# A two-layer hybrid mixer and mixture-of-experts block: the largest expert's three blocks apart, and the first loads of both mixers in places of their own

## The chip, the cores and the metric

The kernel runs on one core of one Trainium2 chip. The metric is the device time of one execution in microseconds (us). Before the change three runs gave 2003.07, 2004.57 and 2011.16 us, a median of 2004.57 us. A difference of about 0.5% (10 us) is what a measurement of this kernel can tell from no change.

## The reference, cut to what matters

512 latent tokens and 256 context tokens of width 1024 go through two layers. Each layer first runs a token mixer: adaptive-norm modulation, one projection into a short convolution and a recurrent head group, one output projection. Then it runs a mixture of 32 experts, of which each token uses two.

```python
for l in range(DEPTH):                                   # 2 layers
    mod = silu(c) @ w_ada[l] + b_ada[l]                  # w_ada[l]: 1024 x 6144
    h = modulate(rms_norm(x, norm_w[l, 0]), mod[0], mod[1])
    y, _, _ = token_mixer(h, w_in[l], ...)               # h @ w_in[l], 1024 x 4096, first
    x = x + mod[2] * (y @ w_out[l])
    h2 = modulate(rms_norm(x, norm_w[l, 1]), mod[3], mod[4])
    f = hier_moe(h2, ..., w_e_gu[l], w_e_down[l])        # per expert: 1024 x 1024 and 512 x 1024
    x = x + mod[5] * f
return rms_norm(x, final_norm_w)
```

The context tokens take the same path in the first layer, so that it routes 768 tokens and the second layer 512. All of it is float32.

## The kernel before, in words

**Order of work.** `run` (L1678) does, per layer, `mixer` (L565), the routing (`route`, L862) and the experts (`moe`, L1469). Each engine has its own queue of instructions. Tile's planner orders them by its own model of their durations, except inside a `manual_schedule` of an engine, where the program's order holds. SP's queue issues most loads and waits in order: a load whose place is not yet free holds up all that stand behind it.

**First layer's start.** `setup` (L40) brings seven small tensors into one 128x128 tile `rows` with seven loads on SP's queue (L47). `norm_first` (L286) loads six tiles of 128 tokens into two places `xin` on ACT's queue, normalises each (ACT's square, POOL's power, DVE's scaling), transposes it on PE (L298) and copies it to `XT`. `ada_step` (L199), eight times, loads 1 MB of `w_ada` on SP's queue into one of three places `adaw` (L215) and multiplies it on PE (L217). From the sum come the modulation's factors `mA` (L241, L242). Then `nat(6)` loads four pieces of `w_in` (0.5 MB each, L317, two places `raw`), and `split_w` (L312) splits each in two: ACT rounds it to the upper part (L319), and POOL or DVE subtracts for the lower part (L322). `modulated` (L264) writes a tile of tokens, again as upper and lower part, into `HA` (input rows 0 to 511) and `HB` (512 to 1023): ACT the upper (L274), DVE the exact value (L278), POOL the difference (L283). `val` (L590) multiplies it by the split weights with 24 matmuls (`proj_N`, L337 to L346) in three kinds per input block: upper by upper, upper by lower weight, lower input by upper weight, block after block. I call these 6 x 24 matmuls the value stage.

**Second layer's start.** The same stage, but the tokens are `X` plus two rows of expert results each, which `combine` (L1615) loads on SP's queue (L1622) and adds on DVE (L1626). DVE keeps the program's order here. Two weight pieces are split with DVE, the other two, loaded between the first `combine` loads, with POOL (L605 to L615).

**Experts.** An expert's weights are six chunks of 1 MB, four of `w_e_gu` and two of `w_e_down`. `ring` (L1168) hands out places in turn from the list `slots`: six of `ra`, eleven of `r0` to `r3`, less one for `m5s` in the first layer, so 16. Three experts are static; the others come by rank of their load in the fixed `order` (L1657). `rooms` (L1653) says for how many tokens a rank has room; `units` (L1456) cuts that into blocks of 128, 64 and 32 tokens. In the first layer rank 0 has 320 (two blocks of 128, one of 64), rank 1 has 192, rank 2 has 128, ranks 3 to 5 have 96, ten ranks 64, thirteen 32. `moe` takes rank after rank: `take_rows` gathers the tokens (POOL's indirect load, PE's transposes), `chunks` does the gate and up matmuls chunk by chunk for all the rank's blocks (L1227 for 128, L1231 else), `end` (L1437) the activation and the down matmuls (L1284, L1296) block by block, and the scatter. PE keeps the program's order. A chunk's place is free when PE has used it for the rank's last block.

```python
order = [[6, 16, 7, 17, 0, 18, 19, 1, 20, 21, 2, 22, 8, 3, 23, 9, ...
def ring(self, n=6):
    pool, name = self.slots.pop(0)
    self.slots.append((pool, name))
```

Of the kernel before, what the change touches and what calls it, by code (L numbers as in the profile page):

```python
# [9 lines left out]
F32 = mybir.dt.float32  # L10
# [9 lines left out]
D = 1024  # L20
# [13 lines left out]
class Backbone:  # L34
# [4 lines left out]
    def setup(self, consts, tmp, ps, dram, stp):  # L39
# [3 lines left out]
        nc.gpsimd.memset(rows, 0.0)  # L43
        q = nc.sync

        def put(r, src):
            q.dma_start(rows[r:r + src.shape[0], :], src)  # L47

        put(0, io["c"].rearrange("a (r j) -> (a r) j", j=128))
        put(8, io["c_ctx"].rearrange("(r j) -> r j", j=128))  # L50
        put(16, io["norm_w"].rearrange("a b (r j) -> (a b r) j", j=128))
        put(48, io["conv_w"].rearrange("a b (r j) -> (a b r) j", j=128))
        put(72, io["conv_norm_w"].rearrange("a (r j) -> (a r) j", j=128))
        put(80, io["hg_lb"].rearrange("a b (r j) -> (a b r) j", j=128))
        put(96, io["hg_norm_w"])
# [143 lines left out]
    def ada_step(self, l, g, k, st, pool, ps, q, bufs):  # L199
# [14 lines left out]
        w = pool.tile([128, 2048], F32, name="adaw", bufs=bufs)  # L214
        q.dma_start(w, io["w_ada"][l, 128 * k:128 * k + 128, 2048 * g:2048 * g + 2048])  # L215
# [47 lines left out]

    def modulated(self, l, i, H, src, pool):  # L264

# [19 lines left out]
    def norm_first(self, H, pool, ps):  # L285

        nc, io = self.nc, self.io
        XT = pool.tile([128, 8, TOK], F32, name="XT")
        for i in range(6):
            xt = pool.tile([128, D], F32, name="xin", bufs=2)  # L290
            src = io["x"][0, i * 128:(i + 1) * 128, :] if i < 4 else io["ctx"][0, (i - 4) * 128:(i - 3) * 128, :]
            nc.scalar.dma_start(xt, src)
            xn = self.normalise(xt, pool)
            for h in range(2):
                pt = ps.tile([128, 512], F32, name="pS", bufs=2)
                for j in range(4):
                    k = 4 * h + j
                    nc.tensor.transpose(pt[:, 128 * j:128 * j + 128], xn[:, 128 * k:128 * k + 128], self.ident)  # L298
# [1527 lines left out]
```

## Time and profile before

| what | value |
|---|---|
| median of three runs | 2004.57 us |
| the profiled execution's own time | 1997.62 us |
| its span, first to last instruction | 1995.8 us |
| busy, share of the span: PE | 1714.4 us, 86% |
| DVE, ACT, POOL | 919.1 us, 456.8 us, 394.1 us |
| mean granted TensorE clock | 0.936 |
| moved by DMA | 542.35 MB, mean 272 GB/s |

The profiled execution is a single one; its time is 6.95 us under the median of the runs. Its span lies 1.8 us under its own time. PE is busy for most of the span, but a busy PE is not PE at its peak, and stages differ: in the expert stages the DMA engines are full, in the mixers they are not. So one reads a stage at a time: which engine or queue runs through it, and which wait ends last. In the rows below a timeline's bracket is the idle time of that engine before the row and what ended it.

### The profile page before, as it was taken

How to read it: one execution, taken by the hardware profiler on the slowest of the kernel's cores; microseconds unless marked ns; L12 is line 12 of the kernel's file. 1: busy time of each engine (PE TensorE's matmuls, PEld its weight loads, DVE VectorE, ACT ScalarE, POOL GpSimd, SP SyncE). 2: the span in 40 equal slices, each digit the busy share in tenths (PEclk: the TensorE clock that was granted, in tenths of full speed). 3: DMA queues.
4: the chain of work that ended last, by engine and by line, in shares of the span. 5: the costliest groups of instructions: out<-in, count | busy, mean ns of one | idle time of the engine just before them, and what ended most of it. 6: DMA issues, size and time to landing. Idle time of an engine off the chain costs nothing. (4 is left out here: it accounts for less than half of the span.)

```text
span 1995.8 us, 33492 instructions
## 1 busy us (share of the span) xinstructions
PE 1714.4 (86%) x13488; PEld 1098.7 (55%) x13488; DVE 919.1 (46%) x2141; ACT 456.8 (23%) x897; POOL 394.1 (20%) x308
## 2 busy tenths in 40 slices
PE   5999899999967999988876799898987898888875
PEld 2766778898844344433322588777764344334342
DVE  4425355634664233222322637666565434355444
ACT  3512223323121122122211533323320100101011
POOL 1501221121112111111110623222212111111110
PEclk8999899999977999998988799999997999999998
DMA  7376563262479979999997422113569989999995
GB/s 276 98 256 229 165 207 97 76 232 83 164 277 416 418 280 390 418 417 417 418 419 319 163 74 65 54 43 91 192 247 375 418 346 400 418 417 417 417 418 246
DMA packets 141512, 542.35 MB, mean 272 GB/s; under 512 B 17393, under 2 KB 66719, under 8 KB 85416
## 3 DMA queue, kind: packets, MB, share of 16 engines
q1 hardware_dynamic: 118408, 466.17, 59.2%
q10 hardware_dynamic: 15040, 55.08, 8.0%
q0 software_dynamic: 7904, 18.90, 2.5%
q8 instruction: 108, 1.77, 0.4%
q14 instruction: 52, 0.43, 0.1%
HBM read 530.95 MB, written 15.96 MB: 274 GB/s over the span
## 5 line engine op out<-in xcount | busy, mean ns | idle before, releaser
L1231 PE MATMUL acc<-w,xT 128*32 128x256 f32 (+1 forms) x3360 | 385.4, 459 | 55.0 <-DMA w<-in_w_e_gu 45.9
L1231 PEld LDWEIGHTS acc<-w,xT 128*32 128x32 f32 (+1 forms) x3360 | 128.5, 121 | 258.3 <-issue 176.3
L322 POOL TENSOR_TENSOR hilo<-raw,hilo 128x1024 fp32r<-128x1024 f32 x64 | 157.5, 2467 | 446.8 <-ACT hilo L319 398.7
L333 PE MATMUL acc<-HA,hilo 128*128 128x384 f32 (+1 forms) x960 | 209.1, 361 | 0.0
L333 PE MATMUL acc<-HB,hilo 128*128 128x384 f32 (+1 forms) x960 | 206.3, 358 | 0.0
L333 PEld LDWEIGHTS acc<-HA,hilo 128*128 128x128 f32 x960 | 172.1, 193 | 16.5 <-issue 4.2
L333 PEld LDWEIGHTS acc<-HB,hilo 128*128 128x128 f32 x960 | 174.3, 194 | 9.5 <-issue 0.8
L345 PE MATMUL acc<-hilo,HA 128*128 128x512 f32 x504 | 131.7, 414 | 13.0 <-ACT HA L274 4.4
L1251 ACT COPY au<-acc 128x256 f32<-128x256 f32 (+1 forms) x69 | 31.2, 452 | 461.6 <-PE acc L1231 439.3
L1190 POOL DMA_INDIRECT xb<-h,idx x63 | 64.2, 1019 | 331.5 <-PE pS L1212 301.8
L345 PE MATMUL acc<-hilo,HB 128*128 128x512 f32 x504 | 125.8, 398 | 3.7 <-DVE hilo L322 3.3
L345 PEld LDWEIGHTS acc<-hilo,HA 128*128 128x128 f32 x504 | 98.1, 199 | 41.6 <-POOL HA L283 5.8
L319 ACT CAST hilo<-raw 128x1024 fp32r<-128x1024 f32 x80 | 83.5, 1049 | 128.2 <-PE acc L345 41.5
L345 PEld LDWEIGHTS acc<-hilo,HB 128*128 128x128 f32 x504 | 94.3, 190 | 29.0 <-issue 4.2
L1182 POOL DMA_INDIRECT yb<-ys,idx x39 | 38.9, 998 | 338.3 <-DVE ys L1298 288.0
L389 DVE TENSOR_TENSOR Q<-Q,Dk 128x256 f32<-128x256 f32 (+1 forms) x144 | 89.8, 653 | 28.8 <-PE pA L435 12.2
L1214 DVE COPY xT<-pS 128x256 f32<-128x256 f32 (+1 forms) x79 | 42.1, 544 | 124.4 <-PE pS L1212 123.6
L1275 DVE SCALAR_TENSOR_TENSOR au<-w,gt,au 32x256 f32<-32x256 f32 (+2 forms) x102 | 58.6, 577 | 60.1 <-ACT au L1274 57.1
L1258 DVE TENSOR_TENSOR hT<-pS,hT 128x128 f32<-128x128 f32 (+1 forms) x69 | 22.9, 340 | 134.3 <-ACT hT L1257 133.9
L384 DVE TENSOR_TENSOR K<-K,Dk 128x768 f32<-128x768 f32 x64 | 72.9, 1139 | 21.8 <-ACT tmp L401 18.3
L1296 PE MATMUL ada<-w,hT 128*32 128x256 f32 (+1 forms) x624 | 67.1, 442 | 5.6 <-issue 4.3
L1334 PE MATMUL ada<-w,hT 128*32 128x256 f32 (+1 forms) x608 | 61.2, 444 | 11.6 <-DVE hT L1259 11.4
(376 smaller groups left out, 2283.8 us busy)
## 6 DMA issues: line engine op xcount, KB each, us to landing
w<-in_w_e_gu SPq DMA_DIRECT2D x242, 1024.0 KB
w<-in_w_e_down SPq DMA_DIRECT2D x121, 1024.0 KB
adaw<-in_w_ada ACTq DMA_DIRECT2D x40, 1024.0 KB
raw<-in_w_in SPq DMA_DIRECT2D x64, 512.0 KB
adaw<-in_w_ada SPq DMA_DIRECT2D x8, 1024.0 KB
raw<-in_w_out SPq DMA_DIRECT2D x16, 512.0 KB
HA<-in_w_e_gu SPq DMA_DIRECT2D x6, 1024.0 KB
h<-SG SPq DMA_DIRECT2D x10, 512.0 KB
```

The source lines that it names most:

```text
L319: nc.scalar.copy(W[:, 0], w)
L322: eng.tensor_sub(W[:, 1], w, W[:, 0].bitcast(F32))
L333: nc.tensor.matmul(o, W[:, wi, k, :], H[k // 4][:, k % 4, hi, t], start=k == 0 and wi == hi, stop=k == 7 and wi == 1)
L345: nc.tensor.matmul(pa, H[k // 4][:, k % 4, hi, t], W[k // 2][:, wi, k % 2, :], start=k == ks[0] and wi == hi, stop=k == ks[-1] and hi == 1)
L384: nc.vector.tensor_tensor(half(Kv, TOK, 0, kn, b), half(Kv, TOK, 0, kn, b), vw(Dv, b, [[2 * b, n], [TOK - b, 2], [0, b]]), op=OP.mult)
L389: nc.vector.tensor_tensor(o, o, vw(Dv, (TOK + b) * d, [[2 * b, qn // (2 * b)], [0, b]]), op=OP.mult)
L1190: self.nc.gpsimd.indirect_dma_start(out=xb, out_offset=None, in_=rows, in_offset=bass.IndirectOffsetOnAxis(ap=idx, axis=0), bounds_check=r ...
L1214: nc.vector.tensor_copy(t[:, :n].rearrange("p a b -> p (a b)"), pt[:, :128 * n])
L1231: nc.tensor.matmul(pg[kind * u:kind * u + kind, :w], xT[k], gu[:, k % 2, w * u:w * u + w], start=st, stop=sp)
L1275: nc.vector.scalar_tensor_tensor(ms[pr, :o], self.m5s[pr, 0, c], g0[pr], ms[pr, :o], op0=OP.mult, op1=OP.add)
L1296: nc.tensor.matmul(py[kind * u:kind * u + kind, :w], hT[k], dn[k // 2][:, k % 2, w * u:w * u + w], start=k == 0, stop=k == 3)
L1334: nc.tensor.matmul(py[pr, :w], hT[k], dn[k // 2][:, k % 2, c], start=k == 0, stop=k == 3)
```

## The change

- `setup`: the seven small tensors are put in one 128x128 array outside the kernel, and one load on ACT's queue brings it.
- First layer's start: the six token tiles get a place each, and the eight pieces of `w_ada` too: six in the memory that later holds `HA` and `HB`, two others. The four pieces of `w_in` get places as well: two in `raw`, two in `SG`. All are issued on SP's queue in one written order: tiles 0 and 1, the eight pieces of `w_ada`, the four of `w_in`, tiles 2 to 5. Tiles 2 to 5 are normalised between the modulations instead of ahead of `ada_step`. DVE and POOL subtract in turn.
- Second layer's start: the four pieces of `w_in` are loaded ahead of all `combine` loads, and DVE splits all four ahead of the first addition. For the first tile DVE, not POOL, subtracts the `HA` half.
- `val`: per half of the input first the eight matmuls with the upper input, then the four with the lower.
- Experts: in the first layer's `order` rank 0 stands three times, one block each, with two ranks between (18 and 19, then 20 and 21), and rank 1 and what follows come later. Its six places are kept out of `slots` until its third block is done.
- `down_here` (second layer only): the result buffer taken is the first that no open group uses, instead of the first of the list.

```diff
-        put(0, io["c"].rearrange("a (r j) -> (a r) j", j=128))
...
-        put(96, io["hg_norm_w"])
+        nc.scalar.dma_start(rows, io["small"])
...
-            nc.gpsimd.tensor_sub(H[h][:, :, 1, sl], mh, H[h][:, :, 0, sl].bitcast(F32))
+            (nc.gpsimd if h else eng or nc.gpsimd).tensor_sub(H[h][:, :, 1, sl], mh, H[h][:, :, 0, sl].bitcast(F32))
...
-    def proj_N(self, W, H, i, ps, group=range(4)):
+    def proj_N(self, W, H, i, ps, group=range(4), high=False):
...
+        ms = [(k, hi, wi) for k in ks for hi, wi in ((0, 0), (0, 1), (1, 0))]
+        if high:
+            ms.sort(key=lambda m: (m[0] // 4, m[1]))
...
+            def early():
+                w = [SG[:, 2 * u - 4:2 * u - 2, :] if u > 1 else
+                     wp.tile([128, 2, 512], F32, name="raw", bufs=self.raw_bufs) for u in range(4)]
+                for u in range(4):
+                    nc.sync.dma_start(w[u], win[256 * u:256 * u + 256, 512 * 6:512 * 7].rearrange("(k p) f -> p k f", p=128))
+                return w
...
+                    with tc.manual_schedule(engines={mybir.EngineType.SP}):
+                        for i in range(2):
+                            nc.sync.dma_start(xin[i], self.token_tile(i))
+                        for k in range(8):
+                            self.ada_load(0, 0, k, aw[k], nc.sync)
+                        ew = early()
+                        for i in range(2, 6):
+                            nc.sync.dma_start(xin[i], self.token_tile(i))
+                    for i in range(2):
+                        self.norm_first(i, xin[i], XT, p0, ps)
                     ast = {}
                     for k in range(8):
-                        self.ada_step(0, 0, k, ast, p0, ps, nc.sync, 3)
+                        self.ada_step(0, 0, k, ast, p0, ps, None, 2, aw[k])
                     self.ada_cols(0)
-                    W = nat(6)
+                    W = [self.split_w(None, wp, True, nc.vector if u % 2 else nc.gpsimd, ew[u]) for u in range(4)]
+                    inputs()
                     for i in range(6):
                         self.modulated(0, i, H, lambda k: XT[:, k, 128 * i:128 * i + 128], p0)
+                        if i + 2 < 6:
+                            self.norm_first(i + 2, xin[i + 2], XT, p0, ps)
                         val(W, i)
                 else:
-                    W = nat(6, range(2), nc.vector)
+                    inputs()
+                    ew = early()
...
                     with tc.manual_schedule(engines={mybir.EngineType.DVE}):
+                        W = [self.split_w(None, wp, True, nc.vector, w) for w in ew]
...
-                            if i == -2:
-                                W += nat(6, range(2, 4), nc.gpsimd)
...
-    def ring(self, n=6):
+    def ring(self, n=6, keep=None):
...
-            self.slots.append((pool, name))
+            (self.slots if keep is None else keep).append((pool, name))
...
-            self.YB.append(self.YB.pop(0))
+            busy = [id(self.into[k]) for k in self.groups if k != kind]
+            self.YB.append(self.YB.pop([id(t) in busy for t in self.YB].index(False)))
...
+        order, units, ends = self.order[l], [], []
+        for n, r in enumerate(order):
+            k, us = order[:n].count(r), self.units(l, r)
+            ends.append(r not in order[n + 1:])
+            units.append(us[k:] if ends[n] else us[k:k + 1])
...
+                if not ends[n]:
+                    kept[r] = []
+                ws[r] = self.load_expert(e, self.ring(keep=kept.get(r)))
...
+            if ends[n]:
+                self.slots += kept.pop(order[n], [])
...
-    order = [[6, 16, 7, 17, 0, 18, 19, 1, 20, 21, 2, 22, 8, 3, 23, 9, 4, 24, 10, 5, 25, 11, 12, 26, 13, 14, 27, 15, 28],
+    order = [[6, 16, 7, 17, 0, 18, 19, 0, 20, 21, 0, 22, 1, 23, 8, 2, 24, 9, 3, 10, 25, 4, 11, 5, 26, 12, 13, 14, 27, 15, 28],
```

## Rows read from the trace of the kernel before

**Rows 1.** Windows of the start: busy us (instructions) per engine, clock, DMA share, GB/s.

```profile
2.00:4.00 2.00, 0.00 (x0) 0.00 (x0) 0.00 (x0) 0.94 (x1) 0.00 (x0) 1.00 0.71 276
...
10.00:20.00 10.00, 9.20 (x33) 3.67 (x33) 6.26 (x35) 3.65 (x7) 1.59 (x3) 1.00 0.97 378
```

**Rows 2.** SP's queue at the start, timeline: start us, us, instruction.

```profile
0.72 0.39 SPq L215 DMA_DIRECT2D adaw<-in_w_ada  x1
...
8.35 25.35 SPq L215 DMA_DIRECT2D adaw<-in_w_ada  x7
```

**Rows 3.** PE at the first layer's start, timeline.

```profile
23.93 1.10 PE L298 MATMUL pS<-ident,xn 128*128 128x128 f32 x8
...
39.09 1.38 PE L217 MATMUL ada<-adaw,sT 128*32 128x512 f32 x8 [2.88 <-DMA adaw<-in_w_ada]
...
46.82 1.22 PE L345 MATMUL acc<-hilo,HA 128*128 128x512 f32 x2 [4.45 <-ACT HA L274]
...
82.66 2.88 PE L345 MATMUL acc<-hilo,HA 128*128 128x512 f32 x12
85.38 2.88 PE L345 MATMUL acc<-hilo,HB 128*128 128x512 f32 x12
```

**Rows 4.** DVE between the last adaptive weights and the modulation, timeline.

```profile
42.58 1.22 DVE L322 TENSOR_TENSOR hilo<-raw,hilo 128x1024 fp32r<-128x1024 f32 x1
43.72 2.31 DVE L241 TENSOR_SCALAR mA<-mc 128x16 f32<-128x16 f32 x1
```

**Rows 5.** Windows of the first value stage, columns as in rows 1.

```profile
47.00:56.00 9.00, 5.69 (x13) 3.66 (x13) 9.00 (x15) 7.05 (x16) 6.18 (x4) 0.65 0.22 60
...
62.00:89.00 27.00, 27.00 (x122) 22.42 (x121) 13.92 (x32) 17.69 (x41) 16.70 (x17) 1.00 0.25 80
```

**Rows 6.** Windows of the first layer's expert stage, columns as in rows 1.

```profile
592.00:700.00 108.00, 93.16 (x834) 44.51 (x827) 39.34 (x122) 18.14 (x39) 21.34 (x20) 0.90 1.01 413
...
710.00:740.00 30.00, 29.81 (x174) 13.17 (x172) 12.34 (x21) 8.57 (x16) 6.01 (x6) 1.00 0.51 187
...
780.00:790.00 10.00, 10.00 (x92) 4.00 (x94) 3.36 (x6) 1.65 (x4) 3.12 (x4) 1.00 0.80 288
790.00:1070.00 280.00, 232.89 (x1664) 92.19 (x1658) 77.45 (x155) 54.17 (x108) 41.60 (x41) 0.93 1.01 418
```

**Rows 7.** PE around the largest expert, timeline.

```profile
678.26 3.60 PE L1227 MATMUL pA<-w,xT 128*128 128x512 f32 x8
...
685.22 1.94 PE L1231 MATMUL acc<-w,xT 128*64 128x512 f32 x8
...
715.54 7.13 PE L1284 MATMUL acc<-w,hT 128*128 128x512 f32 x16 [0.19 <-ACT hT L1246]
...
734.53 1.93 PE L1231 MATMUL acc<-w,xT 128*32 128x256 f32 x32
...
741.70 1.93 PE L1296 MATMUL ada<-w,hT 128*32 128x256 f32 x32 [1.50 <-issue]
```

**Rows 8.** SP's expert loads in the full-rate part, timeline: four chunks of an expert each.

```profile
910.17 9.07 SPq L1163 DMA_DIRECT2D w<-in_w_e_gu  x4
...
926.39 9.47 SPq L1163 DMA_DIRECT2D w<-in_w_e_gu  x4
```

**Rows 9.** The second layer's start, all engines, timeline.

```profile
1094.23 2.54 DVE L322 TENSOR_TENSOR hilo<-raw,hilo 128x1024 fp32r<-128x1024 f32 x2 [1.65 <-ACT hilo L319]
...
1104.08 6.12 POOL L322 TENSOR_TENSOR hilo<-raw,hilo 128x1024 fp32r<-128x1024 f32 x2 [0.17 <-ACT hilo L319]
...
1105.86 5.42 DVE L1626 TENSOR_TENSOR X<-X,y 128x1024 f32<-128x1024 f32 x2 [1.16 <-DMA y<-yb]
...
1108.22 1.22 PE L345 MATMUL acc<-hilo,HA 128*128 128x512 f32 x2 [1.44 <-ACT HA L282]
...
1112.46 4.63 PE L345 MATMUL acc<-hilo,HA 128*128 128x512 f32 x10 [3.02 <-POOL HA L283]
...
1123.29 3.00 PE L345 MATMUL acc<-hilo,HA 128*128 128x512 f32 x12
```

More of the change, by code (lines that the diff above doesn't have):

```diff
@@ L342, in proj_N @@
         ks = [2 * u + a for u in group for a in range(2)]
-        for k in ks:
-            for hi, wi in ((0, 0), (0, 1), (1, 0)):
-                nc.tensor.matmul(pa, H[k // 4][:, k % 4, hi, t], W[k // 2][:, wi, k % 2, :], start=k == ks[0] and wi == hi,
-                                 stop=k == ks[-1] and hi == 1)
+        ms = [(k, hi, wi) for k in ks for hi, wi in ((0, 0), (0, 1), (1, 0))]
+        if high:
+            ms.sort(key=lambda m: (m[0] // 4, m[1]))
+        for m in ms:
+            k, hi, wi = m
+            nc.tensor.matmul(pa, H[k // 4][:, k % 4, hi, t], W[k // 2][:, wi, k % 2, :], start=m == ms[0], stop=m == ms[-1])
         return pa
@@ L576, in mixer, with inputs @@
         with pool("hy", "right") as hy, pool("wp", "right") as wp, pool("sg", "right") as sgp:
-            HA = hy.tile([128, 4, 2, TOK], F32R, name="HA")
+            if l == 0:
+                aw = [t[:, i] for t in (hy.tile([128, 3, 2048], F32, name=n) for n in ("HA", "HB")) for i in range(3)]
             YC = hy.tile([128, 4, TOK], F32, name="YC")
-            HB = hy.tile([128, 4, 2, TOK], F32R, name="HB")
-            H = [HA, HB]
+            def inputs():
+                H[:] = [hy.tile([128, 4, 2, TOK], F32R, name=n) for n in ("HA", "HB")]
+            H = []
             SG = sgp.tile([128, 6, 512], F32, name="SG")
@@ L1474, in moe @@
         self.full = []
-        left = [u[0] for r in self.order[l] for u in self.units(l, r)]
+        order, units, ends = self.order[l], [], []
[3 more added lines that the diff above has]
+            units.append(us[k:] if ends[n] else us[k:k + 1])
+        left = [u[0] for us in units for u in us]
         def flush():
@@ L1482, in flush @@
                     self.complete(kind, ps)
-        order = self.order[l]
         N = len(order)
-        units = [self.units(l, r) for r in order]
-        ws, xT, pg, done = {}, {}, {}, {}
+        ws, kept, xT, pg, done = {}, {}, {}, {}, {}
         def load(n):
-            if n not in ws:
-                r = order[n]
+            r = order[n]
+            if r not in ws:
                 e = nc.sync.value_load(self.eid[0:1, r:r + 1], min_val=32 * l, max_val=32 * l + 31)
-                ws[n] = self.load_expert(e, self.ring())
+                if not ends[n]:
+                    kept[r] = []
+                ws[r] = self.load_expert(e, self.ring(keep=kept.get(r)))
         def rows(n):
@@ L1504, in chunks @@
                 pg[n] = self.sums(units[n], ps)
-            self.chunks(ws[n], units[n], xT[n], pg[n], range(done.get(n, 0), k))
+            self.chunks(ws[order[n]], units[n], xT[n], pg[n], range(done.get(n, 0), k))
             done[n] = k
@@ L1526, in moe @@
                 chunks(n + 1, 1)
-            self.end((ws[n], units[n], pg[n]), mp, ps, n == N - 1, (lambda: chunks(n + 1, k)) if k else None)
+            self.end((ws[order[n]], units[n], pg[n]), mp, ps, n == N - 1, (lambda: chunks(n + 1, k)) if k else None)
+            if ends[n]:
+                self.slots += kept.pop(order[n], [])
             if l:
```

69 lines of the change are left out of this document (35 added, 34 removed).

## The prediction

> **What bounds the kernel now.** I read the windows of the whole span first: a stage with DMA near 418 GB/s is bound by loads, one with PE always busy at full clock by PE. Then I read SP's queue, then PE's and DVE's timelines, in the three stages that the change touches.
>
> *The first layer's start* is bound by loads, and not at full rate. The last matmuls on the adaptive weights begin at 39.09 us, behind a DMA [rows 3]; the loads moved 378 GB/s in the window before [rows 1], 418 being what the queues reach elsewhere [rows 6], because SP issues one piece of `w_ada` at 0.72 us and the other seven only between 8.35 and 33.70 [rows 2], each as one of three places comes free. The value stage begins at 46.82. Its last two groups of 12 matmuls start at 82.66 and 85.38, so 12 take 2.72 us where they follow one another and 144 take 32.6, but the stage took 41.3 (46.82 to 85.38 + 2.72 = 88.1) [rows 3]. Its early part runs at a granted clock of 0.65, its rest at 1.00 [rows 5].
>
> *The first layer's expert stage* is bound by loads: 413 GB/s and 418 GB/s over most of it. But for 30 us the rate falls to 187, and for another 10 us to 288, while PE is busy for 29.81 of the 30 and for all of the 10 [rows 6]. That is the largest expert, and then the next largest: PE works on one rank for so long that no place comes free.
>
> *The second layer's start* is bound by a chain through DVE and POOL. POOL's two weight splits take 6.12 us, and two additions on DVE beside them take 5.42 us, 2.7 each, where two DVE instructions of that size with POOL idle take 2.54; PE then waits 3.02 us for POOL's `HA` [rows 9].
>
> **The experts.** What is lost now: 30 x (1 - 187/418) = 16.6 us, and 10 x (1 - 288/418) = 3.1 us, 19.7 us in all [rows 6]. No byte is added: rank 0 is loaded once. Loads then set the stage's end, so each us of DMA pause that goes is a us of the stage. Does a new pause come? One expert's loads take 16.2 us (926.39 - 910.17) [rows 8]. PE's work on a 128 block: four chunks at 3.6, down 7.1, transposes and activation about 2, some 23.5 us; on a 32 block: gate and up 4 x 0.95 (1.93 for two chunks), down 1.93, transposes 1, some 7; on a 64 block: 4 x 1.94, twice the 32's down, transposes, some 13 [rows 7]. In the new order a 128 block and two 32s are 37.5 us of PE against 32.4 of loads, twice; then the 64 block and rank 22 are 20 against 16.2. So PE falls 5 + 5 + 4 = 14 us behind over the stretch. With six places kept, ten go round: six for the expert that is being used and four, 10.8 us of loads, ahead, and places come free chunk by chunk. That is close, so I leave room for a pause of about 2 us. Rank 1 (36 us) comes when all 16 places are back. **Term: -18 us, from -8 (a lag of 14 that turns into pauses for the most part) to -20.** No instruction is added: each block's gather and scatter on POOL move with it, and SP issues the same chunks in another order; what covers a block's gather is PE's work on the rank before, and if that were too short it would cost a wait of some 2 us.
>
> **The first layer's start.** Loads first. Ahead of the last `w_ada` piece now stand two token tiles and eight pieces, 1.05 + 8.39 = 9.44 MB. The flow starts at about 2.6 us (a share of 0.71 in 2 to 4) [rows 1]; at 418 [rows 6] it takes 22.6 us, to 25.2; with 1.3 us for landing and wait, an estimate, the last matmuls begin at 26.5 instead of 39.09: -12.6. At 378 [rows 1] they would begin at 28.9: -10.2. The order on SP costs nothing: 18 issues at 0.39 [rows 2] are 7 us of a queue that is else idle, and faster than their transfers. Seven small loads on SP become one on ACT, whose first use is not late today.
>
> The Trainium skill, "DMA: Bandwidth & Descriptors", Specifications, gives a limit of about 358 GB/s from HBM for a core; by it the 9.44 MB would take 26.4 us, and the term would lose 3.8. This trace speaks against that limit here: 418 GB/s over 280 us [rows 6].
>
> Then the chain from the last matmuls to the first of the value stage, 7.7 us now (39.09 to 46.82) [rows 3]. In it `mA` takes 2.31 us on 16 elements per lane, beside a split on POOL, and a DVE split of 1.22 stands ahead of it [rows 4]. The new splits fall into the same time, since `w_in` lands from 26 to 31 us, so I take only 1.5 off; the bounds are 0 and 3.3. The value stage begins at about 32.7.
>
> The stage itself: 32.6 us of matmuls, plus the transposes of four token tiles that now stand between them, 4 x 1.1 [rows 3] = 4.4. What is lost at its head was 8.7 (41.3 - 32.6): waits for weight splits and for POOL's half, and the low clock of 0.65 [rows 5]. All four pieces are now there before the stage, and the upper-first order gives PE eight matmuls before it needs POOL, but the clock starts low again after the gap behind `w_ada`: I take 4 us. So 41 us, as before, and it ends at 73.7 instead of 88.1. Tiles 2 to 5 land by (9.44 + 2.10 + 2.10) / 0.418 + 2.6 = 35.2 us; a tile is needed each 6.5 us, so they are covered but for the first, which is 1 to 4 us late if PE's queue has its transposes ahead of tile 0. **Term: -14 us, from -8 to -19.** What follows waits for PE, so it passes on; the first weight place comes free four matmuls later than before (0.9 us), which can cost up to that once a layer.
>
> **The second layer's start.** Two more splits on DVE are 2.5 us, put into the 2 to 3 us in which DVE waits for `y`; what queues behind them are the additions, so if `w_in` lands late they cost as much. POOL's 6.12 us go away, the additions fall from 2.7 to about 1.3 each, the first `HA` difference moves to DVE (0.6, half of a split) and the wait of 3.02 goes [rows 9]. But ACT's square and DVE's chain for tile 1 stand there next, so not all of the 15.1 us from the first matmul to tile 1 (1108.22 to 1123.29) shrinks. Steady tiles follow at PE's pace. **Term: -3 us, from 0 to -6.** The buffer choice in `down_here` issues nothing.
>
> **Sum.** -18 - 14 - 3 = -35 us. Against the profiled execution's own 1997.62 us that is 1962.6. That execution lies 6.95 us under the median of the runs, so I put the same -35 on 2004.57: 1969.6, in round numbers 1969.5 us. The bounds add to -16 and -45: 1988.6 and 1959.6.
>
> **Rivals.**
> *The pauses move.* Ten places are too few and each lag of PE becomes a pause: the experts give 6 instead of 18, the whole -23, 1981.5 us. For it: PE is slower than the loads in that stretch by 14 us. Against: PE comes to rank 0 with no lag, having waited for loads just before (93.16 busy of 108) [rows 6]. 0.17.
>
> *The start is hidden.* PE's and ACT's orders, which the planner makes, put tile 2's work ahead of tile 0's, and the first stage gains 6 instead of 14: -27, 1977.5 us. For it: ACT has four splits, squares and modulation in the same 10 us. 0.12.
>
> *Slower: the value stages run at the low clock.* In the stage's head the granted clock was 0.65, and PE had been waiting in pieces before; it is 1.00 once PE is busy without a break [rows 5]. If the interleaved transposes and squares leave PE waiting before each tile, it stays at 1.2 GHz. A matmul then takes twice 0.227, 0.227 more; 35 / 0.227 = 154 of the 288 matmuls in the two stages must be slow for the gain to be gone. All of them, with transposes, would turn some 41 + 43 us into 74 + 78, +68: 2037 us. Against: even now, with waits, PE reached 1.00 by 62 us. 0.02. The Trainium skill's "TensorE: Matmul & The Clock Gate", in the section "HAM oscillation — how this bites in real kernels", speaks for this one: waits between bursts bring each burst back to a slow start. The trace agrees for the stage's head alone.
>
> *It does not do what it says.* The early loads are held up on SP, and the kept places are the ones next needed: 0, 2004.6 us. The order on SP is written out, so 0.02.
>
> **How the numbers follow.** The forecast has 0.67, the rivals 0.17, 0.12, 0.02 and 0.02. The predicted time is the forecast's. The range takes in the first two rivals and the bounds of the terms, 1958 to 1988. About 0.5%, 10 us, is what can be told from no change. The forecast and the first two rivals are all faster by more than that; leaving 0.02 for their far tails, faster has 0.94, same 0.03, slower 0.03.
>
> **What would show it.** In the changed profile: the last `w_ada` matmuls at 26 to 29 us; the first matmul behind the value stage at 72 to 77; no window of the expert stage under 400 GB/s, with three turns of rank 0; the expert stage's first loads about 14 us earlier; no POOL split after the first additions of the second layer. I am wrong if the last `w_ada` matmuls come after 32 us, if a stretch of 10 us under 300 GB/s is left, or if tile 1 of the second layer starts no earlier against the last expert's scatter.

## The result, and the profile after

| | before | after |
|---|---|---|
| median of four runs | 2005.91 us | 1983.29 us (1981.18 to 1985.85) |
| ratio, with its 95% interval | | 0.9898 [0.9877, 0.9918] |
| the profiled execution, its span | 1997.62, 1995.8 us | 1981.18, 1979.4 us |
| mean granted TensorE clock | 0.936 | 0.942 |

The kernel became faster by 22.6 us (1.0%; its interval is 16 to 25 us), where 35 were forecast: 1983.29 us lies 13.8 us above the forecast of 1969.5 and inside the range of 1958 to 1988. The two profiled executions differ by 16.4 us. Line numbers move in the changed kernel: the value stage's matmuls are L340 and the first matmul behind the stage L324, the adaptive weights L209, the weight split L313, the modulation L266 (ACT) and L270 (DVE), the down matmuls L1320, the expert loads L1187, SP's load of `m5s` L1806, that of `y` L1655.

Milestones of the two traces, in us from the span's start:

| | before | after | difference |
|---|---|---|---|
| last `w_ada` matmuls begin | 39.09 | 26.11 | -13.0 |
| first value stage begins | 46.82 | 31.80 | -15.0 |
| first value stage ends | 88.1 | 80.15 | -8.0 |
| `m5s` load, head of the expert stage | 590.44 | 576.52 | -13.9 |
| last down matrix's load | 1064.93 | 1047.91 | -17.0 |
| last down matmul ends | 1092.08 | 1078.49 | -13.6 |
| second value stage ends | 1153.94 | 1138.30 | -15.6 |

The start, as PE's timeline of the changed kernel shows it [rows 3 of before]:

```profile
26.11 1.07 PE L209 MATMUL ada<-adaw,sT 128*32 128x512 f32 x8 [1.44 <-DMA adaw<-in_w_ada]
...
31.80 2.98 PE L340 MATMUL acc<-hilo,HA 128*128 128x512 f32 x5 [3.10 <-ACT HA L266]
38.07 3.36 PE L340 MATMUL acc<-hilo,HA 128*128 128x512 f32 x7 [3.29 <-DVE hilo L313]
...
44.60 1.07 PE L289 MATMUL pS<-ident,xn 128*128 128x128 f32 x8 [0.62 <-DVE xn L253]
...
49.54 1.07 PE L289 MATMUL pS<-ident,xn 128*128 128x128 f32 x8 [0.43 <-DVE xn L253]
...
56.44 1.06 PE L289 MATMUL pS<-ident,xn 128*128 128x128 f32 x8 [2.18 <-DVE xn L253]
...
77.43 2.88 PE L340 MATMUL acc<-hilo,HB 128*128 128x512 f32 x12
80.15 2.64 PE L324 MATMUL acc<-HA,hilo 128*128 128x384 f32 x12
```

The loads did what was said: 13 us sooner. But the stage, which then began 15 us sooner, lasted 48.4 us instead of 41.3. Its second row of matmuls stands behind DVE's weight split. DVE's timeline says why:

```profile
29.03 1.92 DVE L233 TENSOR_SCALAR mA<-mc 128x16 f32<-128x16 f32 x1
...
31.19 5.69 DVE L270 TENSOR_SCALAR mod<-XT,mA,mc 128x128 f32<-128x128 f32 x9
36.80 1.21 DVE L313 TENSOR_TENSOR hilo<-raw,hilo 128x1024 fp32r<-128x1024 f32 x1
...
39.93 1.21 DVE L313 TENSOR_TENSOR hilo<-SG,hilo 128x1024 fp32r<-128x1024 f32 x1
```

And POOL's timeline beside it:

```profile
28.57 2.35 POOL L313 TENSOR_TENSOR hilo<-raw,hilo 128x1024 fp32r<-128x1024 f32 x1 [19.75 <-ACT hilo L310]
31.29 2.36 POOL L313 TENSOR_TENSOR hilo<-SG,hilo 128x1024 fp32r<-128x1024 f32 x1 [0.37 <-ACT hilo L310]
```

The planner put nine modulations ahead of the second piece's split, and two of the nine were drawn out beside POOL: the one that began at 31.19 lasted 2.54 us and ended 0.08 us after POOL's second split, one at 34.67 lasted 1.44 us beside POOL's difference for `HA`; the other seven took 0.34 us each. Windows of the changed kernel (columns as in rows 1) show the loads at full rate, then the low clock at the head of the stage, then the expert stage:

```profile
4.00:14.00 10.00, 2.44 (x9) 1.75 (x9) 4.67 (x33) 4.13 (x8) 1.84 (x3) 1.00 1.02 426
14.00:24.00 10.00, 9.58 (x60) 3.44 (x64) 2.50 (x6) 0.00 (x0) 0.00 (x0) 1.00 1.01 421
...
31.80:38.00 6.20, 2.87 (x5) 1.33 (x5) 6.20 (x11) 6.20 (x15) 4.30 (x3) 0.50 0.97 344
38.00:45.00 7.00, 6.31 (x17) 4.56 (x18) 5.73 (x11) 2.58 (x6) 4.04 (x4) 0.55 0.27 78
45.00:80.00 35.00, 32.26 (x157) 26.31 (x155) 20.47 (x54) 19.67 (x43) 16.02 (x19) 1.00 0.18 61
...
590.00:600.00 10.00, 8.71 (x125) 4.88 (x129) 6.29 (x16) 5.71 (x13) 2.03 (x2) 0.83 0.33 114
600.00:700.00 100.00, 81.56 (x604) 37.30 (x600) 32.61 (x101) 15.38 (x31) 19.30 (x19) 0.88 1.01 417
700.00:730.00 30.00, 28.02 (x178) 13.14 (x168) 7.85 (x15) 5.21 (x10) 4.08 (x4) 0.90 1.02 418
730.00:740.00 10.00, 9.76 (x70) 4.44 (x70) 1.90 (x4) 0.87 (x3) 3.02 (x3) 0.98 0.88 341
740.00:750.00 10.00, 8.37 (x99) 3.95 (x100) 4.21 (x10) 3.32 (x8) 2.03 (x2) 1.00 0.98 384
...
770.00:780.00 10.00, 10.00 (x34) 3.91 (x32) 2.49 (x6) 2.68 (x6) 0.17 (x1) 1.00 0.76 309
780.00:790.00 10.00, 10.00 (x61) 3.92 (x58) 0.85 (x2) 0.00 (x0) 1.58 (x2) 1.00 0.67 206
790.00:1050.00 260.00, 226.07 (x1473) 88.79 (x1475) 75.00 (x142) 52.50 (x100) 39.02 (x39) 0.95 1.01 418
```

The long pause of rows 6 is gone: 710 to 730 runs at full rate. Smaller ones stay at 730 to 750 and, in rank 1's turn, at 770 to 790. And there is a new one at the head, 590 to 600 at 114 GB/s. SP's timeline there:

```profile
576.52 0.80 SPq L1806 DMA_DIRECT2D w<-modr  x2
578.38 3.88 SPq L1187 DMA_DIRECT2D w<-in_w_e_gu  x4
597.26 0.87 SPq L1187 DMA_DIRECT2D w<-in_w_e_down  x2
```

SP's waits in the same stretch (who waited for whom: us in total, times, longest):

```profile
SPq L1187 <- PE acc L1320: 14.8, 1, 14.8
```

And what it waited for, on PE's timeline:

```profile
595.26 1.93 PE L1320 MATMUL acc<-HB,hT 128*32 128x256 f32 x32 [1.02 <-DVE hT L1283]
```

SP issued four chunks and then held the fifth for 14.8 us, until PE had done the down matmuls of a static expert whose matrix lay in `HB`. Before, SP issued six within 6.3 us, with no wait above 2.0 us:

```profile
592.28 4.86 SPq L1163 DMA_DIRECT2D w<-in_w_e_gu  x4
597.68 0.87 SPq L1163 DMA_DIRECT2D w<-in_w_e_down  x2
```

The change moves `HA` and `HB` together and `YC` behind them in the first layer; the places `r0` to `r2`, which overlay this memory, kept their order.

The second layer's start, all engines [rows 9]:

```profile
1079.05 0.88 SPq L597 DMA_DIRECT2D SG<-in_w_in  x2
1079.26 1.72 POOL L1206 DMA_INDIRECT yb<-ys,idx  x1 [11.73 <-DVE ys L1322]
...
1084.26 16.11 SPq L1655 DMA_DIRECT2D y<-yb  x7
...
1106.81 1.07 PE L340 MATMUL acc<-hilo,HA 128*128 128x512 f32 x4
```

And before, the last scatter and the first load of `y`:

```profile
1092.85 0.98 POOL L1182 DMA_INDIRECT yb<-ys,idx  x1 [11.75 <-DVE ys L1298]
1095.25 0.82 SPq L1622 DMA_DIRECT2D y<-yb  x2
```

Tile 1 comes 27.55 us after the last scatter (1106.81 - 1079.26), against 30.4 before (1123.29 - 1092.85). But `y` is loaded 5.0 us after it, against 2.4. Two weight loads, held until 1079.05 because the last expert still used `SG`, ran beside the scatter; whether they are what delayed `y` is taken up with `f3_weights_elsewhere`.

### The profile page after: what moved, and what is told of

The parts are those of the page before. It is cut to its first block, busy times and chain, and to the rows that moved or that the text cites. A ratio compares the mean times of both kernels' runs of the same rounds, so it can differ in the third digit from the quotient of the medians.

```text
span 1979.4 us, 33460 instructions
## 1 busy us (share of the span) xinstructions
PE 1701.3 (86%) x13487; PEld 1088.9 (55%) x13488; DVE 913.7 (46%) x2144; ACT 458.2 (23%) x897; POOL 387.5 (20%) x304
## 3 DMA queue, kind: packets, MB, share of 16 engines
q1 hardware_dynamic: 119104, 469.27, 59.9%
## 5 line engine op out<-in xcount | busy, mean ns | idle before, releaser
L313 POOL TENSOR_TENSOR hilo<-raw,hilo 128x1024 fp32r<-128x1024 f32 x61 | 149.1, 2447 | 445.7 <-ACT hilo L310 404.8
L324 PE MATMUL acc<-HA,hilo 128*128 128x384 f32 (+1 forms) x960 | 205.3, 355 | 0.2
L324 PE MATMUL acc<-HB,hilo 128*128 128x384 f32 (+1 forms) x960 | 200.8, 351 | 0.0
L324 PEld LDWEIGHTS acc<-HA,hilo 128*128 128x128 f32 x960 | 168.8, 190 | 17.9 <-issue 5.0
L324 PEld LDWEIGHTS acc<-HB,hilo 128*128 128x128 f32 x960 | 169.6, 189 | 9.4 <-issue 0.8
L340 PE MATMUL acc<-hilo,HA 128*128 128x512 f32 x504 | 131.4, 410 | 12.2 <-DVE hilo L313 3.3
L340 PE MATMUL acc<-hilo,HB 128*128 128x512 f32 x504 | 124.4, 396 | 0.6 <-DVE hilo L313 0.6
L340 PEld LDWEIGHTS acc<-hilo,HA 128*128 128x128 f32 x504 | 96.3, 196 | 41.1 <-issue 5.7
L310 ACT CAST hilo<-raw 128x1024 fp32r<-128x1024 f32 x76 | 79.4, 1052 | 129.7 <-PE acc L340 42.7
L340 PEld LDWEIGHTS acc<-hilo,HB 128*128 128x128 f32 x504 | 94.3, 190 | 24.2 <-issue 4.2
L1320 PE MATMUL ada<-w,hT 128*32 128x256 f32 (+1 forms) x656 | 70.6, 451 | 10.3 <-DVE hT L1283 5.9
L1251 PE MATMUL pA<-w,xT 128*128 128x512 f32 x160 | 74.8, 611 | 3.0 <-DMA w<-in_w_e_gu 3.0
```

The source lines that it names most:

```text
L310: nc.scalar.copy(W[:, 0], w)
L313: eng.tensor_sub(W[:, 1], w, W[:, 0].bitcast(F32))
L324: nc.tensor.matmul(o, W[:, wi, k, :], H[k // 4][:, k % 4, hi, t], start=k == 0 and wi == hi, stop=k == 7 and wi == 1)
L340: nc.tensor.matmul(pa, H[k // 4][:, k % 4, hi, t], W[k // 2][:, wi, k % 2, :], start=m == ms[0], stop=m == ms[-1])
L1251: nc.tensor.matmul(pg[u], xT[k], gu[:, k % 2, 512 * u:512 * u + 512], start=st, stop=sp)
L1320: nc.tensor.matmul(py[kind * u:kind * u + kind, :w], hT[k], dn[k // 2][:, k % 2, w * u:w * u + w], start=k == 0, stop=k == 3)
```

## The experiments

The kernel before took 1994.5 to 2006.1 us on the four chips used for the experiments, so each run is given as a ratio to the kernel before on its own chip. The times in the expectations are meant against the 2006 us of the first comparison. Two spans of one trace stand beside each ratio: **expert loads**, from the `m5s` load to the last down matrix's load (before 474.5 us, changed kernel 471.4), and the end of the first **value stage** (88.1 and 80.15). Both scatter too. The changed kernel's expert loads took 471.4 us in one trace and 466.2 in another; the value stage ended at 88.1 and 89.98 in two traces with the old start, and at 80.15, 80.50, 81.43 and 81.55 in four with the changed one. Between that end and the `m5s` load fourteen traces took 495 to 503 us, and before (502.3) and `e2_turns_only` (496.0), which have the same code there, are near the two ends of it.

### One part at a time

**e1_layout**, the changed kernel with the old memory order:

```diff
-                aw = [t[:, i] for t in (hy.tile([128, 3, 2048], F32, name=n) for n in ("HA", "HB")) for i in range(3)]
+                aw = [hy.tile([128, 3, 2048], F32, name="HA")]
             YC = hy.tile([128, 4, TOK], F32, name="YC")
+            if l == 0:
+                aw.append(hy.tile([128, 3, 2048], F32, name="HB"))
+                aw = [t[:, i] for t in aw for i in range(3)]
```

> The changed kernel with one edit: in the first layer the memory behind HA, YC and HB is in the order of the kernel before (HA, YC, HB) instead of HA, HB, YC. Theory: the changed kernel's SP queue waits 13 us for two places at the head of the expert stage (four chunks from 578.38, the next two only at 597.26, with 114 GB/s from 590 to 600) because those places now lie on HB, where the second static expert's down weights are read until 597.2. With the old order that wait goes: no window of 10 us between 585 and 605 under 290 GB/s, and the whole 5 to 8 us faster than the changed kernel, about 1977 us. Rival: the wait comes from the routing or the static experts' own pace; then the window stays near 114 GB/s and the time at 1983 us.

Ratio 0.9901 [0.9877, 0.9925]; expert loads 461.0 us, 590 to 600 at 422 GB/s: the pause is gone, as the theory had it, and the loads are 10.4 and 5.2 us shorter than in the changed kernel's two traces. But the whole is not 5 to 8 us faster: the ratio is that of the changed kernel (0.9898). The value stage ended at 83.4. The waits of SP's queue in its first 20 us show the price of the old order:

```profile
SPq L188 <- DVE lbo L78: 11.1, 1, 11.1
```

And the windows:

```profile
4.00:12.00 8.00, 2.44 (x9) 1.75 (x9) 2.81 (x16) 3.80 (x6) 1.84 (x3) 1.00 1.03 430
12.00:16.00 4.00, 1.72 (x8) 1.57 (x8) 3.54 (x23) 0.32 (x2) 0.00 (x0) 1.00 0.38 100
16.00:28.00 12.00, 7.98 (x58) 1.55 (x56) 0.82 (x2) 0.00 (x0) 0.00 (x0) 1.00 0.99 411
```

There `HB` overlays memory that `setup`'s last operations on DVE read until 14.3 us; SP waits for them with the fourth piece, and the flow breaks off for 4 us. So the new order buys 2 to 3 us at the start (83.27 to 83.45 in three traces with the old order, 80.15 to 81.55 with the new) and loses more than that in the expert loads; in the whole time neither shows.

**e2_turns_only**, the kernel before with the three turns and the kept places alone (new `order[0]`, `ring(keep=)`, `moe`, `down_here`).

> The kernel before with the largest expert's three turns alone (order, kept places). Theory from the changed kernel's trace, where 10 us of DMA pause are left of 20: the expert stage gains about 9 us, 1995 to 1998 us against 2006, with windows under 400 GB/s left near rank 0's second turn and in rank 1's. My prediction's own step: -18, about 1988 us, no window under 400 left. Rival, the pauses only move: within 3 us of the kernel before.

Ratio 0.9924 [0.9895, 0.9952], some -15 us, between the 9 of the theory and the 18 of the prediction; expert loads 458.8. Windows:

```profile
590.00:700.00 110.00, 95.17 (x862) 45.40 (x854) 42.56 (x128) 22.76 (x47) 23.40 (x22) 0.91 1.01 416
710.00:740.00 30.00, 28.03 (x177) 12.37 (x175) 7.02 (x14) 4.49 (x9) 5.06 (x5) 0.94 1.01 414
770.00:790.00 20.00, 20.00 (x88) 7.63 (x87) 2.58 (x7) 0.99 (x3) 2.04 (x2) 1.00 0.83 330
```

In the old memory order the turns take the long pause of rank 0 away (710 to 740: 414 GB/s, before 187); rank 1's is left.

**e3_one_turn**, the changed kernel with the old `order[0]`.

> The changed kernel with the old order of experts, so the largest in one turn, all else as changed. Theory: the three turns are worth 9 us and the pause at the head of the stage stays: 1990 to 1994 us. Rival, the turns are worth nothing within the changed kernel: 1983 us; by my prediction's step, 2001 us.

Ratio 0.9958 [0.9937, 0.9978]; expert loads 477.9, 3.4 more than before, with the wait at the head again (15.7 us for the down matmul). Against the changed kernel's 0.9898 and 0.9914 (`f1_changed_again`) the turns are worth some 9 to 12 us there, near the theory's 9, though the ratio itself lies above the 0.992 to 0.994 that its times come to.

**e4_start_only**, the kernel before with the first layer's start alone, in the old memory order.

> The kernel before with the first layer's start alone (early loads, small tensors in one load, the split from places of their own, upper-first order in the first layer), in the old memory order HA, YC, HB, with the old expert order and the old second-layer start. Theory: the last adaptive weights come 13 us earlier, but the value stage is 7 us longer, since DVE's splits stand behind its modulation; the stage's end and so the whole gain 8 us, 1996 to 1999 us. My prediction's step: -14, about 1992 us.

Ratio 0.9981 [0.9961, 1.0001]; value stage's end 83.4, expert loads 473.0. By the ratio the start is worth some 4 us, with an interval of 0 to 8 whose far end is the theory's figure, in the old memory order, where the flow breaks off as in `e1_layout`; by the end of the changed kernel's stage it is worth 8, not 14. With and without the turns, in the old order, loads take 458.8 and 461.0 against 474.5 and 473.0: the turns are worth 13.9 us (means of two traces each).

### The changed kernel again, and two repairs that missed

**f1_changed_again** is the changed kernel itself.

> The changed kernel itself, unaltered, beside the kernels that follow. If the places of HA, YC and HB are what e1_layout gave back, it stands again at a ratio of 0.990 to 0.991 to the kernel before, its loads pause again for 8 us or more at the head of the first layer's expert stage, and its expert loads last about 471 us from the m5s load to the last down matrix (e1_layout: 461). Rival (the pause was a chance of one execution): 461 to 465 us and no window under 250 GB/s at the head of the stage. It also tells whether the 6 us by which its lead grew between the value stage (7.9 us) and the expert stage (13.9 us) belong to the change: if so, the expert stage begins at 576 to 577 us again; if they were the granted clock of one execution, it may begin anywhere from 576 to 583.

Ratio 0.9914 [0.9885, 0.9944], expert loads 466.2, value stage's end 80.5; 590 to 600 at 110 GB/s:

```profile
590.00:600.00 10.00, 8.75 (x126) 4.81 (x130) 6.40 (x17) 5.73 (x13) 2.03 (x2) 0.83 0.31 110
730.00:750.00 20.00, 18.68 (x197) 8.25 (x197) 7.88 (x18) 5.23 (x12) 5.04 (x5) 1.00 1.00 406
770.00:790.00 20.00, 20.00 (x94) 7.38 (x94) 2.52 (x6) 0.87 (x2) 2.04 (x2) 1.00 0.81 324
```

The pause at the head belongs to the kernel; the one at 730 to 750 comes and goes. The loads lie between the two expectations. The `m5s` load is at 576.1 again, which both of its readings allow; the scatter above is what speaks against an effect of the change on the mixer.

**f2_dve_written**, `e1_layout` with DVE's order written out over the whole first value stage:

```diff
-                    W = [self.split_w(None, wp, True, nc.vector if u % 2 else nc.gpsimd, ew[u]) for u in range(4)]
...
+                    with tc.manual_schedule(engines={mybir.EngineType.DVE}):
+                        W = [self.split_w(None, wp, True, nc.vector if u % 2 else nc.gpsimd, ew[u]) for u in range(4)]
+                        for i in range(6):
+                            self.modulated(0, i, H, lambda k: XT[:, k, 128 * i:128 * i + 128], p0)
...
```

> e1_layout, with DVE's order in the first layer's value stage as written: the two weight splits of DVE ahead of the modulation of tile 0. Theory (the stage lost its gain because the splits stood behind 5.7 us of modulation, and the third and fourth piece of the weights came late to tile 0): the value stage ends some 4 us earlier than in e1_layout (83.4 us), at 79 to 80. Rival (tile 0's delay is made up later, because PE then waits for the square and the normalised rows of tile 2 and what follows): 82 to 84 us, within 1 us of e1_layout.

Ratio 0.9924 [0.9896, 0.9951]; the stage ended at 85.5, 2 us later. Tile 0 took 11.9 us instead of 14.3, but PE then waited for the normalised rows of tiles 2 to 5 (1.2, 2.0, 0.7 and 2.2 us, against 1.3, 0.4, 2.1 and 0.2 in `e1_layout`), and behind the second of these waits the granted clock was 0.61 from 54.5 to 58.6 us. The rival was right, and more.

**f3_weights_elsewhere**, `e1_layout` with the second layer's third and fourth piece in `YC` instead of `SG`.

> e1_layout, with the second layer's third and fourth piece of the first weights loaded into YC's place instead of SG's. Theory (SP waited 7 us for SG's place, which the last expert still used; the two loads then ran beside the last expert's scatter, and the loads of y came 5.0 us after it instead of 2.4): SP no longer waits there, and from the last expert's down matmul to the end of the second value stage it takes about 57.5 us instead of 60.0. Rival (YC's place comes free no sooner, or y waits for the scatter by itself): 59.5 to 60.5 us.

Ratio 0.9910 [0.9879, 0.9941]; SP's wait for the last expert went, yet from the last down matmul to the stage's end it took 61.1 us (60.0). In this execution PE finished the last expert 26.3 us after the last load, in `e1_layout` 29.5; the weights, always issued some 23 us after that load, were then what came late (DVE waited 5.6 us for `raw`). A miss. The first load of `y` came 5.75 us after the scatter, with no load in `SG` beside it, though the four weight loads were issued 1.5 to 3.5 us ahead of it: over the fourteen traces that delay is 2.4 us in three (before, `e4_start_only`, `f4_all`) and 3.1 to 5.8 in the others, and what sets it was not isolated.

**f4_all**, both edits, and rank 1 in two turns (`0, 22, 1, 23, 24, 1, 8, 2, 9, ...`).

> e1_layout with both edits (DVE's written order in the first value stage, second layer's weights elsewhere), and with the second largest expert of the first layer in two turns as well (a block of 128, then 23 and 24, then a block of 64). Theory (what is left of the pauses, 5.9 us in e1_layout at 770 to 790 us, belongs to that expert's long turn): no window of the expert stage under 330 GB/s after the head, its loads last 455 us instead of 461, and with 4 us and 2.5 us from the other two edits the kernel is 12 us below e1_layout, a ratio near 0.984 to the kernel before. Rival (the lag turns into a pause in another place, since six places are kept for two turns more): 459 us or more, and a ratio of 0.987 or above.

Ratio 0.9886 [0.9853, 0.9919]; expert loads 457.0, last down matmul to stage's end 57.1. The loads lie between theory and rival, and the second layer's start gained as the theory had it. The DVE order cost its 2 us at the first value stage again (85.4), and the whole stayed at the rival's ratio.

### Both advantages at once

**g1_places**, the changed kernel with another order of the places:

```diff
-                                        self.slots = ra[:4] + r1 + r2 + r0[2:] + r3[:1] + ra[4:] + r0[:2] + r3[1:]
+                                        self.slots = ra[:4] + r1[:1] + r2 + r0[2:] + r1[1:] + r3[:1] + ra[4:] + r0[:2] + r3[1:]
```

> The changed kernel, whose early adaptive weights keep the early places of HA and HB, with another order of the places that the first layer's experts take in turn: the two that lie on HB, which a fixed expert reads until about 597 us, come after three that do not. Nothing else differs, and no engine's order changes. Theory (the pause at the head of the expert stage is SP waiting for HB's place at the fifth chunk, and the memory order gains 3 us at the start): the value stage still ends at 80 to 81 us, no window between 590 and 620 us is under 380 GB/s, and from the m5s load to the last down matrix it takes 459 to 462 us as in the kernels with the old memory order; the ratio to the kernel before is 0.986 to 0.987. Rival (PE, not SP, sets the pace there, and what is loaded early waits later): 466 to 471 us and a ratio of 0.990 or 0.991.

Ratio 0.9865 [0.9842, 0.9888]; value stage's end 81.6, expert loads 465.2. Six chunks go out within 6.1 us, but the seventh (`r0[2]`, also on `HB`) still waits 11.5 us, and the window of 600 to 610 falls to 350 GB/s. The ratio is the theory's. The loads, just under the rival's 466, are only 1.0 us below the changed kernel's second trace: what the ratio gained is not shown to come from them.

**g2_split_first**, `g1_places` with DVE's order written for tiles 0 and 1 alone (split, tile 0, split, tile 1).

> g1_places, with DVE's order written out for the first two tiles of the first value stage alone: the split of the second weight piece, the modulation of tile 0, the split of the fourth piece, the modulation of tile 1; the planner orders the rest, in another way than before. Theory (tile 0 waits 3.3 us at the low clock for the second piece's split, which stood behind 5.7 us of modulation): tile 0's 24 matmuls end 3 us earlier against the last adaptive weights, and the stage ends 2 to 3 us earlier than in g1_places, at 77.5 to 78.5. Rival (as f2_dve_written showed, what tile 0 gains is lost at the square and the normalised rows of tiles 2 to 5): 80 us or later.

Ratio 0.9865 [0.9842, 0.9888], the same as that of `g1_places`; the stage ended at 79.3, 2.3 us sooner than there and between theory and rival; tile 0's matmuls end at 41.1 instead of 47.1 on PE's timeline:

```profile
31.99 3.57 PE L340 MATMUL acc<-hilo,HA 128*128 128x512 f32 x8 [2.69 <-ACT HA L266]
37.16 1.20 PE L340 MATMUL acc<-hilo,HA 128*128 128x512 f32 x4 [1.61 <-POOL HA L275]
38.20 3.05 PE L340 MATMUL acc<-hilo,HB 128*128 128x512 f32 x12
41.09 1.75 PE L340 MATMUL acc<-hilo,HA 128*128 128x512 f32 x7
45.73 1.94 PE L289 MATMUL pS<-ident,xn 128*128 128x128 f32 x8 [2.89 <-DVE rs L240]
```

Of the 6 us of tile 0, about 1.6 stay: three traces with this order of DVE end the stage at 79.2 to 79.3, four with the changed kernel's at 80.15 to 81.55, 80.9 in the mean. PE now runs eight matmuls before it needs POOL, as the prediction had it; then tile 2's normalised rows come late.

**g3_all**, `g2_split_first` with `YC` for the second layer's weights and rank 1 in two turns.

> g2_split_first, with the second layer's third and fourth weight piece in YC's place and the second largest expert of the first layer in two turns, as in f4_all. Theory (each of these was worth 2 to 4 us in f4_all: last down matmul to the end of the second value stage 57.1 us, expert loads 457.0 us): 57 us and 456 to 458 us here too, 6 us below g2_split_first, a ratio near 0.983 to the kernel before. Rival (f4_all's gain was the order that the planner gave SP by chance, as f3_weights_elsewhere with the same place gained nothing): 60 us for the second value stage, and the whole within 3 us of g2_split_first.

Ratio 0.9851 [0.9825, 0.9878]; expert loads 462.4, last down matmul to the stage's end 58.6, both between theory and rival; the whole is within 3 us of `g2_split_first`, as the rival said. The seventh load still waits 11.5 us.

**h1_all_places**, `g3_all` with the places that lie on `HB` behind three that earlier static experts give back:

```diff
-                                        self.slots = ra[:4] + r1[:1] + r2 + r0[2:] + r1[1:] + r3[:1] + ra[4:] + r0[:2] + r3[1:]
+                                        self.slots = ra[:4] + r1[:1] + r2 + r3[:1] + ra[4:] + r0 + r1[1:] + r3[1:]
```

> g3_all, with one more order of the first layer's places: behind the six that are free at once come three that earlier fixed experts give back (at about 593 us), and only then those that lie on HB, which is read until about 602 us. Theory (in g3_all the seventh load waited 11.5 us for HB, longer than the six before it lasted): SP's longest wait for a down matmul between 588 and 610 us is under 8 us at the seventh load, no window between 590 and 620 us is under 390 GB/s, the expert loads last 458 to 460 us from the m5s load to the last down matrix instead of 462.4, and the ratio to the kernel before is 0.983 to 0.984. Rival (what is gained at the head is lost at the long turns, since PE falls further behind the loads): 462 us or more and a ratio of 0.985 or above.

1972.17 us against 2003.02 on the same chip, ratio 0.9840 [0.9817, 0.9862]; expert loads 459.1. SP's longest wait there fell to 4.8 us, and the head runs at full rate:

```profile
590.00:600.00 10.00, 7.09 (x114) 4.13 (x107) 6.25 (x17) 5.78 (x14) 3.08 (x3) 1.00 1.01 421
600.00:610.00 10.00, 4.45 (x81) 3.13 (x79) 6.93 (x39) 1.74 (x4) 5.11 (x6) 0.76 1.02 416
610.00:620.00 10.00, 7.38 (x83) 5.33 (x84) 5.20 (x25) 0.00 (x0) 2.71 (x3) 0.50 1.01 411
```

All that the theory said came out. Its interval lies below both of the changed kernel's (0.9877 and 0.9885 upward): 1.6% off the kernel before, against 1.0 and 0.9. It beats both kernels. What the last step alone adds to `g3_all` (0.9851) is 2 us by the ratio, within the intervals.

## Why the prediction was right or wrong

**The experts, -18.** The mechanism held: turns with kept places take away the pause, and PE's lag does not bring it back as a whole. The term was mis-sized: 13.9 us (`e1_layout`, `e2_turns_only` against before, `e4_start_only`), since the pause in rank 1's turn, 20 us at 330 GB/s in `e2_turns_only` (4.2 us lost against 418), was to go and stayed. Ten places were enough for rank 0, but for the 0.6 and 2.7 us that the changed kernel's two traces lose at 730 to 750, where 2 were allowed; "rank 1 (36 us) comes when all 16 places are back" was no protection, as its own turn is longer than the loads that fit ahead: ten places at the prediction's 2.7 us a chunk are 27 us. With two turns for it the loads are shorter by 1.8 to 4.0 us in `f4_all` (457.0 against 458.8 to 461.0) and by 2.0 in `g3_all` (against 464.4 in `g2_split_first`); two traces of the changed kernel differ by more (471.4 and 466.2).

**What no step had.** The memory order of `HA`, `HB` and `YC` was in the diff, and the prediction used `HA` and `HB` as a place for early loads only. It also decides which of the experts' places come free last. With the new order, expert loads are 8.9 us longer in the mean where rank 0 has three turns (471.4 and 466.2 against 461.0, 458.8, 461.0 and 458.8) and 4.1 longer where it has one (477.9 against 474.5 and 473.0). `e1_layout`, one edit, shows the cause: with the old order the wait of 14.8 us and the window at 114 GB/s are gone. `h1_all_places` keeps the new order and moves the places instead: against `g3_all` SP's longest wait falls from 11.5 to 4.8 us and the loads from 462.4 to 459.1 us. So by these loads the changed kernel's experts gave some 6 us (3.1 and 8.3 in its two traces) instead of 18. That is the figure of the rival *The pauses move*, whose 1981.5 us is near the 1983.29 measured; its mechanism, too few places round rank 0, is not what cost them, so that agreement is chance.

**The first layer's start, -14.** The loads were forecast well: last `w_ada` matmuls at 26.5, measured 26.11; stage begun at 32.7, measured 31.80. The 1.3 us for landing and wait in that sum stands in no row; only the sum is borne out. And places were not all that held the loads back before: SP's queue stood 4.2 us among the seven small loads, for a token tile's transfer, ahead of the second piece at 8.35. The step that failed is "all four pieces are now there before the stage" and with it the 4 us of loss. They had landed, and ACT had rounded the last by 32.68, but they were not split: DVE's two splits stood at 36.80 and 39.93, behind modulation. The stage lasted 48.4 us and the start gave 8.0. By PE's rows above the first five matmuls cost 6.3 us (31.80 to 38.07) where five at full speed are 1.1, and the next thirteen 6.5 instead of 3.0 at a clock of 0.55; two later waits for normalised rows (0.43 at 49.54, 2.18 at 56.44) are another 2.6. That is 11.3 us where the forecast had 4. *The start is hidden* named the gain (6) and the planner as its cause, but the wrong engines: it was DVE's order. `g2_split_first` confirms that in part: tile 0 is done 6 us sooner and about 1.6 us stay to the stage's end with two tiles' order written out, while the order of the whole stage (`f2_dve_written`) loses 2. How the rest divides between DVE's order, POOL and the clock is open.

On DVE the row of `mA` carries a second lesson. It ended at 30.95, and POOL's split beside it at 30.92; in `e1_layout` the same `mA` took 0.58 us, and ended at 34.31 with POOL at 34.28. The Trainium skill, "SBUF — State Buffer", section "SBUF: two separate sides", says that POOL and some kinds of DVE operation share one pair of ports by an exclusive lock, so that the later one stands until the other's instruction is over. The traces agree to 0.03 us, in before too (46.03 and 46.00). So POOL's work costs DVE's modulation time, which the forecast 41 us did not count: of the nine modulations at 31.19, the two that met POOL's instructions took 2.54 and 1.44 us and ended 0.08 us after these, while the seven with POOL idle took 0.34 each, and the three at 41.07 took 0.33. By the recorded starts the two had begun 0.10 and 0.06 us ahead of POOL, which the trace does not explain. No run takes the splits off POOL, so what this cost the stage was not measured by itself.

**The second layer's start, -3.** From the last down matmul to the end of the value stage: 61.9 us in before, 62.5 and 61.7 in the two kernels with the old start, 59.8 and 59.9 in the changed one: -2, inside 0 to -6. POOL's splits left the chain as forecast; what was not forecast is `y`, loaded 5.0 us after the scatter instead of 2.4. Whether another place is better stayed unclear: 61.1, 57.1, 58.6 and 59.5 us in the four kernels with `YC`.

**The sum.** From -35, 6 are lost at the start, 4 in the turns, 9 to the places and 1 in the second layer: -15, against 16.4 between the two profiled executions. The median's 22.6 has an interval of 16 to 25 us, and `f1_changed_again` gives 17. What lies between was not taken apart; a single execution scatters by as much. So the range was met with some luck: two of the three terms came out at or past the small end of their own bounds (-8.0 at the start, about -6 for the experts), and the -15 that they add up to, put on 2004.57, would be 1989.6 us, just outside it. *Slower* (low clock throughout) did not come: 0.50 to 0.55 until 45 us, then 1.00.

Of the signs named ahead, the last `w_ada` matmuls (26.11) came as said. The stage's end (80.15 for 72 to 77) and the windows under 400 GB/s did not. The expert stage's first loads came 13.9 us earlier, as said, but only 8.0 of that stood at the end of the value stage; the rest is no more than the mixer behind it scatters.

The first "wrong if" holds off (26.11 against 32 us), so does the third (tile 1 is 2.9 us nearer the scatter); the second struck: a window of 114 GB/s at the head, and one of 206.

The prediction weighed the limit of 358 GB/s in the Trainium skill's "DMA: Bandwidth & Descriptors", Specifications, against the trace's 418. The changed kernel settles it for a core by itself: 421 to 426 GB/s from 4 to 24 us. The Trainium skill's "Perfetto Trace Analysis", section "Roofline", says that a single active core may exceed that share, up to some 435 GB/s of its 16 DMA engines; the runs agree.

## What to carry to other kernels

When early loads are put into memory that something else uses later, list every later tenant: the order in which tiles lie there also decides in which order places come free, and a load queue that waits in order turns one late place into a stall for all behind it. Rotate the places in the order in which they are given back, not in that of their names. An operand is ready when its last helper is done, not when its load lands: look up on which engine the helper stands, and behind what.

## What was not expected

- One piece of setup on DVE (`lbo`, 0.16 us long) held a load of 1 MB for 11.1 us, by its place alone (`e1_layout`).
- The same down matmuls near the stage's end took 6.60 us in the changed kernel's trace and 3.65 in `g1_places`'s, by the granted clock; from the last load to the last down matmul it took 25.2 to 30.6 us, whatever the kernel.
- The first load of `y` came 2.4 to 5.8 us after the last expert's scatter, over the fourteen traces. Moving two weight loads out of its way (`f3_weights_elsewhere`) did not shorten it.
